# A third seven-product unit pair for the first panel pairs of two down-projection parts

## Chip, core and metric

One core of one Trainium2 chip runs the kernel, with its engines PE (matmul), DVE and ACT (elementwise work) and the queues that issue transfers. The metric is device time in microseconds (us) of the whole launch.

## What is computed

A decoder trunk of two layers on 256 tokens of width 2048, everything in float32. Each layer mixes tokens (gated linear attention, then forgetting attention, both with cross-attention to 256 memory tokens) and ends in a gated MLP with a short convolution. The change lies in the MLP's second product, `@ w_down`:

```python
FFN_HIDDEN = 11 * D_MODEL // 4          # 5632

def conv_ffn(h, w_up, conv_w, conv_b, w_down):
    u = causal_dwconv(h @ w_up, conv_w, conv_b)
    a, val = split_cols(u, [FFN_HIDDEN, FFN_HIDDEN])
    return (jax.nn.silu(a) * val) @ w_down

# per layer i, after the mixer
h = rmsnorm(x, norm_ffn[i])
x = x + conv_ffn(h, ffn_w_up[i], ffn_conv_w[i], ffn_conv_b[i], ffn_w_down[i])
```

## The kernel before

**Precision by halves.** A float32 factor is split into a high half (`hi`, rounded to the type fp32r) and the rest (`lo`). A product of two such factors is three matmuls: token high by weight high, token low by weight high, token high by weight low. Each matmul has a 128x128 block of activations (one chunk of 128 channels, one half of the tokens) as stationary operand, and moves 512 columns of weights.

**Units and panels.** Weights lie in memory as panels of 512 output columns, each cut into units of two chunks: 128 x 1024 values, 512 KB. For each unit, SP's queue loads `raw` (four buffers, line 207), ACT rounds it into `whi` (three buffers, line 208), and DVE subtracts to get `wlo` (three buffers, line 217). Then PE runs the products. `passed()` counts units and runs delayed steps that are due.

**The MLP.** The 5632 hidden channels go in three parts of 16, 16 and 12 chunks (`PARTS`). For each part, up panels are multiplied first; each result is scaled by ACT, turned through device memory, and eight to nine units later `taken` does the convolution and gating and splits the channel's activations into the chunk buffers (`A` in layer 0, `B` in layer 1, tiles 0 to 15). Then come four down panels over the part's 16 chunks, so eight units each.

**Seven products instead of eight.** In the first two parts, the down panels go in pairs (f = 0, 1 and f = 2, 3) through `add_seven` and `proj_seven`. A unit of both panels of the pair (a unit pair) is a 2x2 block product: two token halves, two chunks, two panels. Done plainly it is eight block products, 24 matmuls. In the units listed in `SEVEN`, a scheme of seven products replaces it, 21 matmuls. It needs sums of weights: from the two raw tiles `r0`, `r1` of the unit pair, DVE makes `t13` and `t24` (lines 338 to 341), and `halves` splits `r0`, the second half of `r1`, `t13` and `t24` (called v0, v1, v2, v3 below; the halves of v1 are `vhi` and `vlo`). It needs sums of activations too (`forms`, made by `summed`, lines 1021 to 1031, from `sf`), which are made for every unit that is in `SEVEN[1]`. Four of the seven products have one place each in the result and share the accumulators m1, m5, m6, m7 over all seven-product units of the pair (`ps_t`, `ps_s`, `ps_o`, `ps_s` in PSUM); the other three add into the ordinary accumulators `acc`. At the pair's end, DVE adds the four `acc` and, in `more`, the combinations of the m's to the residual `x`. There are eight banks: four for `acc`, four for the m's.

**What sets the order.** Every engine runs its own list in order, and waits at semaphores. The order of the lists is made ahead by a scheduler, from program order and priorities: loads and splits are raised by `AHEAD`, raw sums by `AHEAD + 40`, so that weights are prepared before the matmuls that use them. It interleaves the units of neighbouring panels.

## Time and profile before

| | us |
|---|---|
| median of 3 runs | 2243.26 (2242.03 to 2243.55) |
| the profiled execution | 2244.32 |
| its span | 2242.5 |
| DVE busy | 1631.0 |
| ACT busy | 1288.8 |

A busy share is an average over the whole span. Whether a helper engine holds PE up is read at one place, from the order of the lists and the start times there.

### The profile page before, as it was taken

How to read it: one execution, taken by the hardware profiler on the slowest of the kernel's cores; microseconds unless marked ns; L12 is line 12 of the kernel's file. 1: busy time of each engine (PE TensorE's matmuls, PEld its weight loads, DVE VectorE, ACT ScalarE, POOL GpSimd, SP SyncE). 2: the span in 40 equal slices, each digit the busy share in tenths (PEclk: the TensorE clock that was granted, in tenths of full speed). 3: DMA queues.
4: the chain of work that ended last, by engine and by line, in shares of the span. 5: the costliest groups of instructions: out<-in, count | busy, mean ns of one | idle time of the engine just before them, and what ended most of it. 6: DMA issues, size and time to landing. Idle time of an engine off the chain costs nothing.

```text
span 2242.5 us, 29514 instructions
## 1 busy us (share of the span) xinstructions
PE 2229.0 (99%) x10276; PEld 1861.9 (83%) x10276; DVE 1631.0 (73%) x2553; ACT 1288.8 (57%) x1910; POOL 2.9 (0%) x15
## 2 busy tenths in 40 slices
PE   9999999999999999999999999999999999999998
PEld 7888888888888888888888998888888888888886
DVE  7568887667689677886776556666777967797766
ACT  7555666556565566555655555555665455654654
POOL 0000000000000000000000000000000000000000
PEclk9999999999999999999999999999999999999999
DMA  9876667677876777668787986677776678766774
GB/s 320 276 237 189 202 201 229 202 239 242 256 222 200 244 236 244 210 205 249 237 250 249 260 265 205 179 247 236 249 247 208 206 241 243 240 197 229 238 242 150
DMA packets 303773, 516.97 MB, mean 231 GB/s; under 512 B 178556, under 2 KB 187272, under 8 KB 303496
## 3 DMA queue, kind: packets, MB, share of 16 engines
q1 hardware_dynamic: 124296, 427.24, 59.1%
q10 hardware_dynamic: 179328, 87.85, 14.0%
q8 instruction: 80, 1.31, 0.3%
q14 instruction: 69, 0.57, 0.1%
HBM read 470.44 MB, written 44.58 MB: 230 GB/s over the span
## 4 chain that ended last, share of the span: by engine, by line
PE 96%; DMA 1%; DVE 1%; issue 0%; ACT 0%; SPq 0%; ACTq 0%; DVEq 0%
PE acc L229 26%; PE acc L230 26%; PE acc L233 26%; PE acc L291 12%; PE ps_s L291 1%; PE ps_o L291 1%; PE ps_t L291 1%; DMA xturned<-square 1%; PE ps_s L785 0%; DVE wlo L217 0%; PE ps_t L575 0%; PE ps_s L586 0%; PE ps_o L597 0%; DMA mt<-memt 0%; DMA raw<-wp 0%
## 5 line engine op out<-in xcount | busy, mean ns | idle before, releaser
L217 DVE TENSOR_TENSOR wlo<-raw,whi 128x1024 fp32r<-128x1024 f32 (+4 forms) x769 | 921.4, 1201 | 503.4 <-ACT whi L208 459.7
L208 ACT ACTIVATE whi<-raw 128x1024 fp32r<-128x1024 f32 (+4 forms) x769 | 799.0, 1041 | 741.1 <-PE acc L230 528.3
L229 PE MATMUL acc<-whi,B 128*128 128x512 f32 (+3 forms) x1536 | 586.2, 383 | 0.6 <-ACT whi L208 0.6
L230 PE MATMUL acc<-whi,B 128*128 128x512 f32 (+3 forms) x1536 | 584.9, 382 | 0.0
L229 PE MATMUL acc<-whi,A 128*128 128x512 f32 x1184 | 462.5, 392 | 0.9 <-ACT whi L208 0.6
L230 PE MATMUL acc<-whi,A 128*128 128x512 f32 x1184 | 461.2, 391 | 0.0
L233 PE MATMUL acc<-wlo,B 128*128 128x512 f32 (+3 forms) x1536 | 400.7, 381 | 0.0
L229 PEld LDWEIGHTS acc<-whi,B 128*128 128x128 f32 x1536 | 288.2, 188 | 51.5 <-ACT whi L208 1.1
L230 PEld LDWEIGHTS acc<-whi,B 128*128 128x128 f32 x1536 | 287.9, 188 | 49.7
L233 PEld LDWEIGHTS acc<-wlo,B 128*128 128x128 f32 x1536 | 285.6, 188 | 49.8
L233 PE MATMUL acc<-wlo,A 128*128 128x512 f32 x1184 | 318.5, 390 | 0.3 <-DVE wlo L217 0.3
L229 PEld LDWEIGHTS acc<-whi,A 128*128 128x128 f32 x1184 | 222.1, 188 | 49.2 <-ACT whi L208 2.4
L233 PEld LDWEIGHTS acc<-wlo,A 128*128 128x128 f32 x1184 | 222.1, 188 | 46.9 <-DVE wlo L217 0.7
L230 PEld LDWEIGHTS acc<-whi,A 128*128 128x128 f32 x1184 | 222.2, 188 | 46.1 <-DVE A L479 0.4
L1010 ACT ACTIVATE cv<-u,cw 128x256 f32<-128x256 f32 x176 | 96.8, 588 | 21.0 <-DMA u<-turned 21.0
L291 PE MATMUL acc<-whi,B 128*128 128x512 f32 x392 | 102.9, 390 | 0.3 <-ACT whi L208 0.3
L291 PE MATMUL acc<-whi,A 128*128 128x512 f32 x392 | 103.0, 390 | 0.0
L1011 DVE SCALAR_TENSOR_TENSOR cv<-u,cw,cv 128x256 f32<-128x256 f32 x176 | 78.4, 480 | 12.9 <-ACT cv L1010 12.9
L291 PEld LDWEIGHTS acc<-whi,B 128*128 128x128 f32 x392 | 73.5, 188 | 16.4 <-ACT whi L208 0.8
L291 PEld LDWEIGHTS acc<-whi,A 128*128 128x128 f32 x392 | 73.5, 188 | 16.1 <-ACT whi L208 0.4
L312 ACT ACTIVATE whi<-t 128x1024 fp32r<-128x1024 f32 x40 | 42.4, 1061 | 69.0 <-DVE t L341 35.3
L394 DVE STREAM_TRANSPOSE square<-scaled 128x512 f32<-128x512 f32 x122 | 79.9, 691 | 0.0
(231 smaller groups left out, 1604.0 us busy)
## 6 DMA issues: line engine op xcount, KB each, us to landing
raw<-wp SPq DMA_DIRECT2D x743, 512.0 KB, 4.3
turned<-square ACTq DMA_DIRECT2D x61, 512.0 KB, 4.3
u<-turned ACTq DMA_DIRECT2D x176, 128.0 KB, 5.1
raw<-wp SPq DMA_DIRECT2D x32, 384.0 KB, 3.5
raw<-wp SPq DMA_DIRECT2D x24, 388.0 KB, 4.6
back<-xturned ACTq DMA_DIRECT2D x64, 128.0 KB, 5.3
xturned<-square ACTq DMA_DIRECT2D x12, 512.0 KB, 4.0
back<-turned ACTq DMA_DIRECT2D x32, 128.0 KB, 4.6
```

The lines of the kernel that those rows point to most:

```text
L208: casts.append(S.activation(hi[:, s], raw[:, s], AF.Copy))
L217: V.tensor_tensor(lo[:, s], raw[:, s], hi[:, s].bitcast(F32), ALU.subtract)
L229: TE.matmul(acc[:, :n], xh, hi[:, s], start=first and j == 0, stop=False)
L230: TE.matmul(acc[:, :n], xl, hi[:, s], start=False, stop=False)
L233: TE.matmul(a, xh, ls, start=False, stop=stop)
L291: TE.matmul(a, x, w, start=k not in begun, stop=calls[k] == 0)
L312: casts.append(S.activation(hi, raw, AF.Copy))
L394: V.transpose(self.square[:, :, :, b], src.rearrange("p (c t) -> p c t", t=32))
L1010: S.activation(r, v[:, 2:], AF.Identity, bias=w[3], scale=w[2])
L1011: V.scalar_tensor_tensor(r, v[:, 1 : T + 1], w[1], r, ALU.mult, ALU.add)
```

## The change

`SEVEN` names the units in seven-product form for the first panel pair and for the second. It changes from `((3, 5), (3, 5, 7))` to `((3, 5, 7), (3, 5, 7))`: unit 7, the last of the eight, takes the seven-product form in the first pair also. This concerns two parts in each of two layers, so four places. The rest of the diff makes `proj_seven` work for other widths (`n` in place of 512), makes the shared accumulators when the first seven-product unit needs them, and moves the token sums into `token_sums`. `seven_evacuated`, `sums_of` and the argument `extra` are not used by any call.

```diff
-SEVEN = ((3, 5), (3, 5, 7))
+SEVEN = ((3, 5, 7), (3, 5, 7))
...
-    def proj_seven(keys, src, forms, evacs, pool, more, early=False):
+    def proj_seven(keys, src, forms, evacs, tiles, more, early=False):
...
-        count = len(units[0])
+        count, n = len(units[0]), units[0][0][2]
...
-        m1, m5, m6, m7 = (work(t, n) for t, n in (("t", 1), ("s", 2), ("o", 1), ("s", 2)))
         begun, calls = set(), {}
+        shared = []
...
-                        for b in range(2):
-                            evacs[i](b, acc[i][b])
+                        for b in range(2):
+                            evacs[i](b, acc[i][b][:, :n])
                 if u == count - 2 and count - 1 in forms:
                     evacs[1](1, acc[1][1])
                 continue
+            if not shared:
+                shared += [work(t, m) for t, m in (("t", 1), ("s", 2), ("o", 1), ("s", 2))]
+                for a in shared:
+                    count_calls(a, 3 * len(forms))
+            m1, m5, m6, m7 = shared
             s = forms[u]
             with tc.high_priority(offset=AHEAD + 40):
                 r0, r1 = (load(units[i][u]) for i in range(2))
-                t13, t24 = (pool.tile([P, 2, 512], F32, name=n, tag=n) for n in ("t13", "t24"))
-                V.tensor_tensor(t13[:, 0, :], r1[:, :512], r0[:, :512], ALU.subtract)
-                V.tensor_tensor(t13[:, 1, :], r1[:, 512:], r1[:, :512], ALU.subtract)
-                V.tensor_tensor(t24[:, 0, :], r1[:, 512:], t13[:, 0, :], ALU.subtract)
-                V.tensor_tensor(t24[:, 1, :], r0[:, 512:], t24[:, 0, :], ALU.subtract)
+                t13, t24 = (tiles(t, F32)[:, : 2 * n] for t in ("t13", "t24"))
+                V.tensor_tensor(t13[:, :n], r1[:, :n], r0[:, :n], ALU.subtract)
+                V.tensor_tensor(t13[:, n:], r1[:, n:], r1[:, :n], ALU.subtract)
+                V.tensor_tensor(t24[:, :n], r1[:, n:], t13[:, :n], ALU.subtract)
+                V.tensor_tensor(t24[:, n:], r0[:, n:], t24[:, :n], ALU.subtract)
             with tc.high_priority(offset=AHEAD):
-                v0 = halves(r0, NUNIT)
-                v1 = halves(r1[:, 512:], 512)
+                v0 = halves(r0)
+                v1 = halves(r1[:, n:], True)
             passed()
             emit([form(m1, token(k0, 0), *v0, 0), form(acc[0][0], token(k1, 0), *v0, 1)])
             emit([form(acc[1][0], s(3), *v1, 0)])
...
+    def token_sums(a0, a1, b0, b1, f, form):
+        V.tensor_tensor(f[:, 0, :], a1, b1, ALU.add)
+        V.tensor_tensor(f[:, 2, :], a0, a1, ALU.subtract)
+        V.tensor_tensor(f[:, 1, :], f[:, 0, :], a0, ALU.subtract)
+        V.tensor_tensor(f[:, 3, :], b0, f[:, 1, :], ALU.subtract)
+        hi, lo = form
+        S.activation(hi, f, AF.Copy)
+        V.tensor_tensor(lo, f, hi.bitcast(F32), ALU.subtract)
...
-                        add_seven(key, f, m, {u: form(forms[u]) for u in at}, sp)
+                        add_seven(key, f, m, {u: form(forms[u]) for u in at}, spare_tile)
```

With the old table, the rewritten functions give every engine the same rows in the same order as before. With the new one, the four places change alike. Three lists at the first of them (layer 0, part 0, end of the first panel pair):

**DVE**, from where its list first differs (just behind the split of `A14`). `wlo_6364` and `wlo_6382` belong to unit 6 of both panels, `wlo_6400` and `wlo_6420` to unit 7. Before:

```order
L217 TENSOR_TENSOR wlo_6364<-raw_6360,whi_6361 128x1024
L1026 TENSOR_TENSOR sf_6276<-cv1_6244,cv1_6268 128x128
L217 TENSOR_TENSOR wlo_6382<-raw_6378,whi_6379 128x1024
L476 TENSOR_TENSOR A15_99<-cv1_6268,A15_99 128x256
L1028 TENSOR_TENSOR sf_6276<-sf_6276,cv1_6244 128x128
L217 TENSOR_TENSOR wlo_6400<-raw_6396,whi_6397 128x1024
L1029 TENSOR_TENSOR sf_6276<-cv1_6268,sf_6276 128x128
L217 TENSOR_TENSOR wlo_6420<-raw_6416,whi_6417 128x1024
L1031 TENSOR_TENSOR forms2_4585<-sf_6276,forms2_4585 128x512
```

Now:

```order
L346 TENSOR_TENSOR t13_6401<-raw_6399,raw_6397 128x512
L347 TENSOR_TENSOR t13_6401<-raw_6399 128x512
L217 TENSOR_TENSOR wlo_6364<-raw_6360,whi_6361 128x1024
L315 TENSOR_TENSOR vlo_6412<-raw_6399,vhi_6411 128x512
L400 TENSOR_TENSOR sf_6276<-cv1_6244,cv1_6268 128x128
L217 TENSOR_TENSOR wlo_6382<-raw_6378,whi_6379 128x1024
L348 TENSOR_TENSOR t24_6402<-raw_6399,t13_6401 128x512
L524 TENSOR_TENSOR A15_99<-cv1_6268,A15_99 128x256
L315 TENSOR_TENSOR wlo_6408<-raw_6397,whi_6407 128x1024
L402 TENSOR_TENSOR sf_6276<-sf_6276,cv1_6244 128x128
L315 TENSOR_TENSOR wlo_6425<-t13_6401,whi_6424 128x1024
L349 TENSOR_TENSOR t24_6402<-raw_6397,t24_6402 128x512
```

The raw sums of unit 7 and its extra splits stand among unit 6's splits; the low half of v3 and the forms' low half come behind the rows shown.

**ACT**, from the split of `A14` on. Before:

```order
L475 ACTIVATE A14_98<-cv1_6244 128x256
L208 ACTIVATE whi_6379<-raw_6378 128x1024
L208 ACTIVATE whi_6397<-raw_6396 128x1024
L475 ACTIVATE A15_99<-cv1_6268 128x256
L208 ACTIVATE whi_6417<-raw_6416 128x1024
L208 ACTIVATE whi_6455<-raw_6454 128x1024
L1030 ACTIVATE forms2_4585<-sf_6276 128x512
```

Now (`whi_6407`, `whi_6424`, `whi_6434` are the high halves of v0, v2, v3; `whi_6462` is the next panel pair's unit 0):

```order
L523 ACTIVATE A14_98<-cv1_6244 128x256
L208 ACTIVATE whi_6379<-raw_6378 128x1024
L314 ACTIVATE vhi_6411<-raw_6399 128x512
L314 ACTIVATE whi_6407<-raw_6397 128x1024
L523 ACTIVATE A15_99<-cv1_6268 128x256
L314 ACTIVATE whi_6424<-t13_6401 128x1024
L314 ACTIVATE whi_6434<-t24_6402 128x1024
L208 ACTIVATE whi_6462<-raw_6461 128x1024
L405 ACTIVATE forms2_4585<-sf_6276 128x512
L1021 ACTIVATE s16_6447<-ps_t_6195 128x512
L208 ACTIVATE whi_6480<-raw_6479 128x1024
```

`whi_6434` stands behind DVE's second `t24`, and the next pair's `whi_6462` behind it.

**PE**, unit 6's low products and the start of unit 7. Before:

```order
L291 MATMUL acc_6066<-wlo_6364,A12_96 128x512
L291 MATMUL acc_6066<-wlo_6364,A13_97 128x512
L291 MATMUL acc_6067<-wlo_6364,A12_96 128x512
L291 MATMUL acc_6067<-wlo_6364,A13_97 128x512
L291 MATMUL acc_6066<-whi_6397,A14_98 128x512
L291 MATMUL acc_6066<-whi_6397,A15_99 128x512
L291 MATMUL acc_6067<-whi_6397,A14_98 128x512
L291 MATMUL acc_6067<-whi_6397,A15_99 128x512
L291 MATMUL acc_6066<-whi_6397,A14_98 128x512
L291 MATMUL acc_6067<-whi_6397,A14_98 128x512
L291 MATMUL acc_6068<-wlo_6382,A12_96 128x512
L291 MATMUL acc_6068<-wlo_6382,A13_97 128x512
```

Now; ahead of the rows shown stand, in the place where the list first differs, two matmuls of v0 on `ps_t` and the first one of `wlo_6364`:

```order
L291 MATMUL acc_6066<-wlo_6364,A13_97 128x512
L291 MATMUL acc_6067<-wlo_6364,A12_96 128x512
L291 MATMUL acc_6067<-wlo_6364,A13_97 128x512
L291 MATMUL acc_6066<-whi_6407,A15_99 128x512
L291 MATMUL acc_6068<-wlo_6382,A12_96 128x512
L291 MATMUL acc_6068<-wlo_6382,A13_97 128x512
L291 MATMUL acc_6069<-wlo_6382,A12_96 128x512
L291 MATMUL acc_6069<-wlo_6382,A13_97 128x512
L291 MATMUL acc_6066<-whi_6407,A15_99 128x512
L291 MATMUL ps_t_6195<-wlo_6408,A14_98 128x512
L291 MATMUL acc_6066<-wlo_6408,A15_99 128x512
L291 MATMUL acc_6067<-whi_6434,A15_99 128x512 x2
```

Behind them follow the next panel pair's first eight matmuls, all of `whi_6462`; the seven form's remaining products come after those. So the two matmuls of v3 stand 14 matmuls behind the place where the list first differs.

More of the change, by code (lines that the diff above doesn't have):

```diff
@@ L268, in proj_two @@
                         evacs[i](b, acc[i][b][:, : units[i][0][2]])
-    def proj_seven(keys, src, forms, evacs, pool, more, early=False):
+    def proj_seven(keys, src, forms, evacs, tiles, more, early=False):
         units = [where[k] for k in keys]
-        count = len(units[0])
+        count, n = len(units[0]), units[0][0][2]
         base = min(min(u[1]) for u in units[0])
         acc = [[pacc.tile([P, 512], F32, name="acc", tag="acc") for _ in range(2)] for _ in keys]
-        m1, m5, m6, m7 = (work(t, n) for t, n in (("t", 1), ("s", 2), ("o", 1), ("s", 2)))
         begun, calls = set(), {}
+        shared = []
         def form(a, x, hi, lo, c):
-            s = slice(c * 512, (c + 1) * 512)
+            s = slice(c * n, (c + 1) * n)
             out = []
@@ L290, in emit @@
                 calls[k] -= 1
-                TE.matmul(a, x, w, start=k not in begun, stop=calls[k] == 0)
+                TE.matmul(a[:, :n], x, w, start=k not in begun, stop=calls[k] == 0)
                 begun.add(k)
@@ L300, in proj_seven @@
                 count_calls(acc[i][b], 6 * len(plain))
-        for a in (m1, m5, m6, m7, acc[0][0], acc[1][0], acc[0][1]):
+        for a in (acc[0][0], acc[1][0], acc[0][1]):
             count_calls(a, 3 * len(forms))
@@ L305, in token, with halves @@
             return [src[kc - base][:, i, b * P : (b + 1) * P] for i in range(2)]
-        def halves(raw, w):
-            if w == NUNIT:
-                hi, lo = (wpool.tile([P, w], F32R, name=n, tag=n, bufs=3) for n in ("whi", "wlo"))
-            else:
-                hi, lo = (pool.tile([P, w], F32R, name=n, tag=n) for n in ("vhi", "vlo"))
+        def halves(raw, single=False):
+            w = n if single else 2 * n
+            if single:
+                hi, lo = (tiles(t, F32R) for t in ("vhi", "vlo"))
+            else:
+                hi, lo = (wpool.tile([P, NUNIT], F32R, name=t, tag=t, bufs=3) for t in ("whi", "wlo"))
+            hi, lo = hi[:, :w], lo[:, :w]
             casts.append(S.activation(hi, raw, AF.Copy))
@@ L317, in load @@
             off, kcs, n = unit
-            raw = wpool.tile([P, NUNIT], F32, name="raw", tag="raw", bufs=4)
-            loads.append(nc.sync.dma_start(raw, wp[off : off + P * NUNIT].rearrange("(p n) -> p n", p=P)))
+            w = len(kcs) * n
+            raw = wpool.tile([P, NUNIT], F32, name="raw", tag="raw", bufs=4)[:, :w]
+            loads.append(nc.sync.dma_start(raw, wp[off : off + P * w].rearrange("(p n) -> p n", p=P)))
             return raw
@@ L348, in proj_seven @@
             with tc.high_priority(offset=AHEAD):
-                v2 = halves(t13.rearrange("p c n -> p (c n)"), NUNIT)
+                v2 = halves(t13)
             emit([form(m5, s(0), *v2, 0), form(m7, s(2), *v2, 1)])
             with tc.high_priority(offset=AHEAD):
-                v3 = halves(t24.rearrange("p c n -> p (c n)"), NUNIT)
+                v3 = halves(t24)
             passed()
@@ L362, in proj_seven, with seven_evacuated, more, evac @@
             more(m1, m5, m6, m7)
+    def seven_evacuated(keys, src, forms, evacs, tiles):
+        n = where[keys[0]][0][2]
+        extra = {}
+        def more(m1, m5, m6, m7):
+            u, v, w = (tiles(t, F32)[:, :n] for t in ("s16", "s165", "s1675"))
+            m1, m5, m6, m7 = (m[:, :n] for m in (m1, m5, m6, m7))
+            S.activation(u, m1, AF.Copy)
+            V.tensor_tensor(u, u, m6, ALU.add)
+            V.tensor_tensor(v, u, m5, ALU.add)
+            V.tensor_tensor(u, u, m7, ALU.add)
+            V.tensor_tensor(w, u, m5, ALU.add)
+            extra.update({(0, 0): m1, (1, 0): v, (0, 1): u, (1, 1): w})
+        def evac(i):
+            return lambda b, a: evacs[i](b, a, extra[i, b])
+        proj_seven(keys, src, forms, [evac(i) for i in range(2)], tiles, more, True)
+    def sums_of(src, chunks, f, h, form):
+        for c, k in enumerate(chunks):
+            V.tensor_tensor(h[:, c, :], *(src[k][:, i, :].bitcast(F32) for i in range(2)), ALU.add)
+        (a0, a1), (b0, b1) = ([h[:, c, b * P : (b + 1) * P] for b in range(2)] for c in range(2))
+        token_sums(a0, a1, b0, b1, f, form)
+    def token_sums(a0, a1, b0, b1, f, form):
[6 more added lines that the diff above has]
+        V.tensor_tensor(lo, f, hi.bitcast(F32), ALU.subtract)
     def turned(pool, bank, width, col):
@@ L422, in to_features, with evac @@
         held = []
-        def evac(b, a):
+        def evac(b, a, extra=None):
             if not held:
@@ L435, in evac @@
                     S.activation(o, i, AF.Copy, scale=s()[:, b : b + 1])
+                    if extra is not None:
+                        V.scalar_tensor_tensor(o, extra, s()[:, b : b + 1], o, ALU.mult, ALU.add)
             held[0].put(b, e)
@@ L445, in to_values, with evac @@
         held = []
-        def evac(b, a):
+        def evac(b, a, extra=None):
             e = tp.tile([P, 512], F32, name="scaled", tag="scaled", bufs=2)
             S.activation(e[:, :width], a[:, :width], AF.Copy, scale=norm.col()[:, b : b + 1])
+            if extra is not None:
+                V.scalar_tensor_tensor(e, extra, norm.col()[:, b : b + 1], e, ALU.mult, ALU.add)
             held.append(e)
@@ L965, in add_out, with add_seven @@
             proj_tm((*key, f), src, add_panel(f, then), spare if f == 3 else None)
-    def add_seven(key, f, src, forms, pool, then=None):
+    def add_seven(key, f, src, forms, tiles, then=None):
         x0, x1 = x[f], x[f + 1]
@@ L979, in more @@
             V.tensor_tensor(x1, x1, m5.unsqueeze(1).to_broadcast([P, 2, 512]), ALU.add)
-        proj_seven([(*key, g) for g in (f, f + 1)], src, forms, [add_panel(g, then) for g in (f, f + 1)], pool, more,
+        proj_seven([(*key, g) for g in (f, f + 1)], src, forms, [add_panel(g, then) for g in (f, f + 1)], tiles, more,
                    then is not None)
@@ L997, in ffn, with spare_tile @@
             held = []
+            def spare_tile(name, dtype):
+                return sp.tile([P, 512 if name in ("vhi", "vlo") else NUNIT], dtype, name=name, tag=name)
             def form(t):
@@ L1022, in summed @@
             def summed(form):
-                h0, h1 = (natural(h) for h in held)
+                ab = [natural(h)[:, :, b] for h in held for b in range(2)]
                 held.clear()
-                f = sp.tile([P, 4, P], F32, name="sf", tag="sf")
-                V.tensor_tensor(f[:, 0, :], h0[:, :, 1], h1[:, :, 1], ALU.add)
-                V.tensor_tensor(f[:, 2, :], h0[:, :, 0], h0[:, :, 1], ALU.subtract)
-                V.tensor_tensor(f[:, 1, :], f[:, 0, :], h0[:, :, 0], ALU.subtract)
-                V.tensor_tensor(f[:, 3, :], h1[:, :, 0], f[:, 1, :], ALU.subtract)
-                S.activation(form[:, 0, :, :], f, AF.Copy)
-                V.tensor_tensor(form[:, 1, :, :], f, form[:, 0, :, :].bitcast(F32), ALU.subtract)
+                token_sums(*ab, sp.tile([P, 4, P], F32, name="sf", tag="sf"), [form[:, h, :, :] for h in range(2)])
             def panel(j, base, slack=0):
@@ L1062, in ffn @@
                     for f, at in zip((0, 2), SEVEN):
-                        add_seven(key, f, m, {u: form(forms[u]) for u in at}, sp)
+                        add_seven(key, f, m, {u: form(forms[u]) for u in at}, spare_tile)
                     continue
                 if LAST:
-                    add_seven(key, 0, m, {u: form(forms[u]) for u in LAST}, sp, then)
+                    add_seven(key, 0, m, {u: form(forms[u]) for u in LAST}, spare_tile, then)
                 sums.close()
```

## The prediction

> **What bounds the kernel now.** I read the page first, then PE's waits, then the four places one after another. The page's chain and PE's list of waits (columns: waits in total, count, longest) say:

> ```profile
> PE 2229.0 (99%) x10276; PEld 1861.9 (83%) x10276; DVE 1631.0 (73%) x2553; ACT 1288.8 (57%) x1910; POOL 2.9 (0%) x15
> PE 96%; DMA 1%; DVE 1%; issue 0%; ACT 0%; SPq 0%; ACTq 0%; DVEq 0%
> PE ps_o L174 <- DVE B L171: 1.4, 1, 1.4
> ...
> PE acc L233 <- DVE wlo L217: 0.3, 1, 0.3
> ```

> PE is the whole story: the seven rows of its waits add to 4.1 us of a span of 2242.5. So a matmul taken away is worth its full pitch, and any wait put into PE's list costs its full length, since nothing later gives it back. DVE's 73% is an average; what counts is DVE at the four places. Busy time by stretch (PE, PEld, DVE, ACT) around the end of the first panel pair:

> ```profile
> 664.00:674.00 10.00, 10.00 (x45) 8.07 (x43) 10.00 (x15) 5.93 (x8) 0.00 (x0) 1.00 0.62 208
> 674.00:684.00 10.00, 10.00 (x45) 8.03 (x44) 8.68 (x15) 5.30 (x7) 0.00 (x0) 1.00 0.64 207
> 684.00:694.00 10.00, 10.00 (x46) 8.29 (x45) 10.00 (x14) 4.34 (x5) 0.00 (x0) 1.00 0.67 216
> 922.00:932.00 10.00, 10.00 (x45) 8.23 (x44) 10.00 (x16) 6.38 (x9) 0.00 (x0) 1.00 0.63 205
> 1716.00:1726.00 10.00, 9.44 (x40) 6.88 (x38) 10.00 (x16) 6.12 (x8) 0.00 (x0) 1.00 0.61 209
> 1974.00:1984.00 10.00, 10.00 (x45) 8.23 (x44) 10.00 (x17) 6.40 (x9) 0.00 (x0) 1.00 0.60 209
> ```

> In the ten microseconds ahead of each place DVE is busy without a gap: units 3 and 5 in seven form, and the last up panels' convolution and forms, fall together there. The change puts more DVE work at just that point.

> **What is taken away.** Each place loses 24 - 21 = 3 matmuls. The existing seven-product unit (unit 3 here) and a plain stretch behind it give both prices:

> ```profile
> 658.50 0.39 PE L291 MATMUL ps_t<-whi,A 128*128 128x512 f32 x1
> ...
> 663.36 3.79 PE L291 MATMUL acc<-whi,A 128*128 128x512 f32 x16
> 666.98 1.07 PE L291 MATMUL acc<-wlo,A 128*128 128x512 f32 x4
> ```

> Plain: 16 matmuls in 666.98 - 663.36 = 3.62 us, 0.226 each, so 24 take 5.43. Seven form: its 21 run from 658.50 to 663.36, 4.86. The gain is 0.57 a place, 2.3 us in four places (2.7 if the three are counted at 0.226). This is the most that the change can bring beyond the waits that exist.

> **What is added on DVE, and when PE needs it.** Four raw sums of 512, the 512-wide `vlo`, and three splits of 1024 in place of two. The order of the lists up to the split of `A14` is unchanged, so DVE reaches the first changed instruction when it now starts `wlo_6364`. DVE's list there, and ACT's answer to a second `t24`:

> ```profile
> 668.97 0.69 DVE L341 TENSOR_TENSOR t<-raw,t 128x512 f32<-128x512 f32 x1
> 669.58 1.22 DVE L313 TENSOR_TENSOR wlo<-raw,whi 128x1024 fp32r<-128x1024 f32 x1
> ...
> 674.98 1.23 DVE L217 TENSOR_TENSOR wlo<-raw,whi 128x1024 fp32r<-128x1024 f32 x1
> 676.12 0.29 DVE L1026 TENSOR_TENSOR sf<-cv,cv 128x128 f32<-128x128 f32 x1
> 676.32 1.23 DVE L217 TENSOR_TENSOR wlo<-raw,whi 128x1024 fp32r<-128x1024 f32 x1
> 677.45 0.42 DVE L476 TENSOR_TENSOR A<-cv,A 128x256 fp32r<-128x256 f32 x1
> 677.79 0.29 DVE L1028 TENSOR_TENSOR sf<-sf,cv 128x128 f32<-128x128 f32 x1
> ...
> 669.78 1.06 ACT L312 ACTIVATE whi<-t 128x1024 fp32r<-128x1024 f32 x1 [3.03 <-DVE t L341]
> 673.14 2.20 ACT L208 ACTIVATE whi<-raw 128x1024 fp32r<-128x1024 f32 x2 [0.57 <-PE acc L291]
> ```

> Start to start, a 512-wide one takes 0.61 (668.97 to 669.58), a 1024-wide split 1.13, a 256-wide one 0.34, a 128-wide one 0.20. From 674.98 to the end of the second `t24` the new list has 12 instructions: four splits (4.52), two `t13`, `vlo` and the first `t24` (2.42), two `sf` (0.40), `A15` (0.34), and the last `t24` at its full 0.69. That is 8.37. ACT starts 0.12 behind it (668.97 + 0.69 to 669.78) and rounds v3's high half in 1.06. So `whi_6434` is there 9.55 us behind DVE's start.

> PE reaches the place where its list differs when it now starts unit 6's low products. The four places' two starts:

> ```profile
> 677.61 1.07 PE L291 MATMUL acc<-wlo,A 128*128 128x512 f32 x4
> 932.57 1.22 DVE L217 TENSOR_TENSOR wlo<-raw,whi 128x1024 fp32r<-128x1024 f32 x1
> 935.98 1.07 PE L291 MATMUL acc<-wlo,A 128*128 128x512 f32 x4
> 1726.79 1.23 DVE L217 TENSOR_TENSOR wlo<-raw,whi 128x1024 fp32r<-128x1024 f32 x1
> 1729.40 1.07 PE L291 MATMUL acc<-wlo,B 128*128 128x512 f32 x4
> 1984.32 1.23 DVE L217 TENSOR_TENSOR wlo<-raw,whi 128x1024 fp32r<-128x1024 f32 x1
> 1987.76 1.07 PE L291 MATMUL acc<-wlo,B 128*128 128x512 f32 x4
> ```

> PE is 2.63, 3.41, 2.61 and 3.44 us behind DVE's start, and has 14 matmuls (3.16 us) in front of v3's. It arrives 5.8 to 6.6 us behind DVE's start, and the weights come at 9.55. **First wait:** 3.76, 2.98, 3.78 and 2.95 us, together 13.5. Part of it falls ahead of v3, at `wlo_6408`, which the same DVE list brings late; the sum is the same.

> **Second wait:** ACT rounds `whi_6462` behind `whi_6434`; 1.10 a piece (2.20 for two), against two matmuls of v3 (0.45) in front of it. 0.6 a place, 2.4 us. All matmuls behind these two waits in PE's list are queued, the next pair's eight first, though their accumulators are free.

> **Third:** `whi_6480` (next pair, unit 0, second panel) takes the buffer of v2's high half, which PE holds until the forms' low products are through, so cast, split and DVE's addition of the old accumulator follow each other just when PE asks. From the rows: the cast 1.06 against about three matmuls left, the split's 1.13 against four matmuls, the addition 0.61 against two. Each is short by 0.2 to 0.3: 0.8 a place at most, nothing if the buffer comes free sooner. No row shows it; I take 0.6, 2.4 us, since the first two waits have the same order of work.

> **At nothing:** the forms of unit 7 exist already, for the second pair. Transfers keep their sequence. `r1` of unit 7 must have landed by DVE's first sum:

> ```profile
> 670.82 0.33 SPq L207 DMA_DIRECT2D raw<-wp  x1
> DMA to landing us min/median/max: 3.2/4.1/4.9
> ```

> At the median it lands at 674.9, just in time for 674.98; at the longest 0.7 late, 2.9 us in four places; that end goes into the range. The raw tiles of unit 7 are held until the last `t24`, so the fourth next load starts at about 683.2 and lands four later; PE asks for it after 692. The new placement of the m accumulators and the unused helpers issue nothing.

> [...] The rows' starts are closer together than their durations, so the trace decides against charging them whole.

> **Sum:** 13.5 + 2.4 + 2.4 - 2.3 = +16.0. The profiled execution's own 2244.32 (1.8 outside the span) becomes 2260.3; it lies 1.06 above the median, so I say 2259 for the runs.

> **Rivals.**
> *Not slower: PE has enough in front.* The same DVE list ran for unit 5 in the stretch 664 to 674, DVE full, and PE lost nothing in three of the four places (at 1716 it lost 0.56). If DVE's lead at the place were 6.4 us, in place of 2.6 to 3.4, the first wait would vanish, and the others with it, as ACT would follow: 2243.3 - 2.3 = 2241. Against it: DVE has no gap ahead of the place, so there is no lead to be found. 9%.
> *Half of it:* the waits that follow the first vanish, and some DVE instruction ahead of it is in truth covered: first wait 2 us a place, 8 - 2.3 = +5.7, 2249. For it: small differences of a few tenths in 12 instructions. 8%.
> *PE's clock falls after each wait.* The first matmuls of the launch, behind PE's longest wait, are slow:

> ```profile
> 1.45 3.61 PE L174 MATMUL ps_o<-B 128*128 128x512 f32 x8 [1.45 <-DVE B L171]
> ```

> Eight in 3.61, against 1.81 at 0.226: 1.8 us lost. After each of four waits that is 7.2 more: 2266. Against it, the wait is in two pieces (some 0.9, then 2.0 to 2.7) with matmuls between. 8%. [...]
> *The change does nothing:* the lists show that it does; no chance.

> **How the numbers follow.** Forecast 75%: +12 to +19, from the third wait at nothing and the gain at 2.7 to late loads, so 2255 to 2262 alone. The range reaches to the half case below and to the clock case above: 2249 to 2266. A change of 0.2% (4.5 us) is about what a measurement can tell from none. Slower by more: forecast, clock, and most of the half case, 88%. Within: nearly all of the not-slower case, as its 2.3 us are 0.1%, and a little of the half case, 9%. Faster by more needs the whole gain and PE's existing 4.1 us of waits, 3%.

> **What would show it.** PE's waits grow from 4.1 to about 22 us, led by `acc` of the seven products on ACT's rounding of `t` (v3), with next `ps_t` on the low half of v0, once at each place; PE has 12 matmuls fewer; DVE is full from each place until some 8 us later. No wait of PE on `t`'s rounding would refute the first step; eight slow matmuls after a wait would show the clock; waits on `raw` would show late loads. If these four places show less than 1.5 us of wait each, the forecast is wrong.

## The result and the profile after

The kernel became slower: 2263.49 us (2257.72 to 2266.38 in four runs) against 2242.66 (four runs, one more than in the table ahead), a ratio of 1.0084 with a 95% interval of 1.0073 to 1.0096, so about 21 us. The forecast was 2259. The profiled execution of after is the shortest of the four, 2257.72 us with a span of 2255.9; it is 13.4 us above the profiled one of before. The runs of before lie within 1.5 us, those of after within 8.7. The mean granted clock is 0.997 in the shortest run of after and 0.995 and 0.996 in the two longest; it was 0.999 in before.

The page's line of busy times, its chain by engine, and PE's waits of after (total, count, longest):

```profile
PE 2232.5 (99%) x10264; PEld 1861.8 (83%) x10264; DVE 1646.1 (73%) x2577; ACT 1293.5 (57%) x1918; POOL 2.9 (0%) x15
PE 91%; DVE 4%; DMA 2%; issue 1%; ACT 1%; SPq 0%; ACTq 0%; DVEq 0%
...
PE acc L291 <- ACT whi L314: 9.1, 4, 2.4
PE ps_o L174 <- DVE B L171: 1.4, 1, 1.4
PE acc L229 <- ACT whi L208: 1.3, 3, 0.8
PE acc L291 <- DVE wlo L217: 0.7, 1, 0.7
PE acc L291 <- ACT whi L208: 0.6, 3, 0.2
PE ps_t L291 <- DVE wlo L315: 0.5, 1, 0.5
PE acc L233 <- DVE wlo L217: 0.2, 1, 0.2
```

PE has 12 matmuls fewer. The first row is the forecast's first wait, four times, of `acc` on the rounding of `t`. The chain now passes through DVE, DMA and ACT for 4, 2 and 1%, where before PE had 96%. The first place, row by row (DVE's first raw sum; PE at the point where its list differs; DVE's last raw sum; ACT's rounding of it, and of the next pair's unit; v3's two matmuls; the next pair's first eight):

```profile
673.50 0.69 DVE L346 TENSOR_TENSOR t<-raw 128x512 f32<-128x512 f32 x1 [0.53 <-DVE A L524]
677.11 0.62 PE L291 MATMUL ps_t<-whi,A 128*128 128x512 f32 x2
681.20 0.68 DVE L349 TENSOR_TENSOR t<-raw,t 128x512 f32<-128x512 f32 x1
682.00 1.06 ACT L314 ACTIVATE whi<-t 128x1024 fp32r<-128x1024 f32 x1 [4.04 <-DVE t L349]
682.96 1.04 ACT L208 ACTIVATE whi<-raw 128x1024 fp32r<-128x1024 f32 x1
683.11 0.73 PE L291 MATMUL acc<-whi,A 128*128 128x512 f32 x2 [2.37 <-ACT whi L314]
684.06 2.11 PE L291 MATMUL acc<-whi,A 128*128 128x512 f32 x8 [0.21 <-ACT whi L208]
```

From DVE's first sum to v3's first matmul are 683.11 - 673.50 = 9.61 us; the other three places give 9.61, 9.60 and 9.61. PE comes 3.61 us behind DVE's start (3.07, 4.21, 3.95 at the others). Now the same matmuls at the second and the fourth place, and the stretches around the first, second and fourth (after the busy times: granted clock, DMA share, GB/s):

```profile
944.86 4.22 PE L291 MATMUL acc<-whi,A 128*128 128x512 f32 x10 [2.38 <-ACT whi L314]
...
2002.69 3.48 PE L291 MATMUL acc<-whi,B 128*128 128x512 f32 x8 [0.21 <-ACT whi L208]
```

```profile
674.00:684.00 10.00, 7.47 (x31) 5.16 (x29) 10.00 (x16) 4.48 (x7) 0.00 (x0) 1.00 0.57 186
944.00:954.00 10.00, 9.14 (x32) 7.09 (x33) 7.92 (x12) 5.80 (x7) 0.00 (x0) 0.83 0.39 120
2004.00:2014.00 10.00, 10.00 (x40) 8.05 (x39) 7.54 (x10) 4.41 (x5) 0.00 (x0) 0.88 0.44 114
```

Eight matmuls behind the wait take 2.11 us at the first place and 3.48 at the fourth, and the granted clock of that stretch is 0.88 in place of 1.00. So PE's clock fell at the second (0.83) and the fourth place (0.88), and not at the first and the third (1.00 in 674 to 684 and in 1736 to 1746).

**Where the time went.** I measured in the trace, from the start of the first matmul of a part's two panel pairs to the start of the last, and counted in it PE's waits, and what consecutive starts of 512-column matmuls lie apart beyond 0.2265 us each (waits taken out, differences under 0.01 us left out):

| place | before: stretch, waits, pitch | after: stretch, waits, pitch |
|---|---|---|
| 1 | 84.29, 0, 0.29 | 86.87, 2.58, 0.87 |
| 2 | 84.05, 0, 0 | 88.92, 2.91, 2.60 |
| 3 | 85.36, 0.63, 0.79 | 86.33, 2.27, 0.57 |
| 4 | 84.03, 0, 0 | 89.15, 3.20, 2.48 |

Together the stretches grew by 13.54 us, all of the difference between these two executions. Waits brought 10.96 - 0.63 = 10.3, slower pitch 6.52 - 1.08 = 5.4, the fewer matmuls -2.3: 13.4. Of the pitch, some 0.5 a place is PE starting again after a wait (places 1 and 3); the rest, 1.5 to 2 us each, is the clock at places 2 and 4.

### The profile page after: what moved, and what is told of

Its sections match the earlier page's. It is cut to its first block, busy times and chain, and to the rows that moved or that the text cites. A ratio compares the mean times of both kernels' runs of the same rounds, so it can differ in the third digit from the quotient of the medians.

```text
span 2255.9 us, 29526 instructions
## 1 busy us (share of the span) xinstructions
PE 2232.5 (99%) x10264; PEld 1861.8 (83%) x10264; DVE 1646.1 (73%) x2577; ACT 1293.5 (57%) x1918; POOL 2.9 (0%) x15
## 3 DMA queue, kind: packets, MB, share of 16 engines
q10 hardware_dynamic: 179328, 87.85, 13.8%
## 4 chain that ended last, share of the span: by engine, by line
PE 91%; DVE 4%; DMA 2%; issue 1%; ACT 1%; SPq 0%; ACTq 0%; DVEq 0%
PE acc L229 26%; PE acc L230 26%; PE acc L233 26%; PE acc L291 8%; DVE wlo L217 1%; DMA raw<-wp 1%; PE ps_s L291 1%; DVE wlo L315 1%; DMA xturned<-square 1%; PE ps_s L833 0%; PE ps_o L291 0%; ACT whi L208 0%; DVE vlo L315 0%; PE ps_t L291 0%; PE ps_t L623 0%
## 5 line engine op out<-in xcount | busy, mean ns | idle before, releaser
L217 DVE TENSOR_TENSOR wlo<-raw,whi 128x1024 fp32r<-128x1024 f32 (+4 forms) x761 | 910.4, 1199 | 496.7 <-ACT whi L208 448.9
L208 ACT ACTIVATE whi<-raw 128x1024 fp32r<-128x1024 f32 (+4 forms) x761 | 789.6, 1040 | 713.0 <-PE acc L230 514.8
L233 PE MATMUL acc<-wlo,B 128*128 128x512 f32 (+3 forms) x1536 | 400.6, 381 | 0.0
L233 PEld LDWEIGHTS acc<-wlo,B 128*128 128x128 f32 x1536 | 285.7, 188 | 49.7
L233 PE MATMUL acc<-wlo,A 128*128 128x512 f32 x1184 | 318.5, 390 | 0.2 <-DVE wlo L217 0.2
L233 PEld LDWEIGHTS acc<-wlo,A 128*128 128x128 f32 x1184 | 222.1, 188 | 46.7 <-DVE wlo L217 0.7
L291 PE MATMUL acc<-whi,A 128*128 128x512 f32 x368 | 99.3, 396 | 5.0 <-ACT whi L314 4.8
L291 PE MATMUL acc<-whi,B 128*128 128x512 f32 x368 | 99.4, 396 | 4.8 <-ACT whi L314 4.4
L314 ACT ACTIVATE whi<-t 128x1024 fp32r<-128x1024 f32 x48 | 50.5, 1060 | 90.5 <-DVE t L349 44.7
L291 PEld LDWEIGHTS acc<-whi,A 128*128 128x128 f32 x368 | 69.8, 191 | 21.6 <-ACT whi L314 5.6
L291 PEld LDWEIGHTS acc<-whi,B 128*128 128x128 f32 x368 | 69.6, 190 | 21.4 <-ACT whi L314 5.2
```

The costliest lines, as they stand in the source:

```text
L208: casts.append(S.activation(hi[:, s], raw[:, s], AF.Copy))
L217: V.tensor_tensor(lo[:, s], raw[:, s], hi[:, s].bitcast(F32), ALU.subtract)
L233: TE.matmul(a, xh, ls, start=False, stop=stop)
L291: TE.matmul(a[:, :n], x, w, start=k not in begun, stop=calls[k] == 0)
L314: casts.append(S.activation(hi, raw, AF.Copy))
```

## The experiments

"Before" was run again beside each group of them, at a median of 2243.5 to 2243.7 us, and the ratios are against that. "After" is the changed kernel; each edit is made to it.

### The same kernel again

> The changed kernel once more, for its spread. Theory A (PE waits for the high half of v3, and in some of the four places its clock falls to half for some microseconds afterwards): the runs spread again over some 8 us, 2257 to 2267, and the granted clock of a run, 0.995 to 0.997, is lower the longer it is; the profile shows a first wait of 2 to 3.4 us in each place and eight to ten slow matmuls behind some of them. Rival B (the spread comes from loads that land early or late): the clock doesn't go with the time, and the profile shows waits on raw tiles.

Measured: 2264.8 us (2263.0 to 2265.62), ratio 1.0096 (1.0081 to 1.0112). The profiled execution is longer than that of after by 5.3 us. Its four places, v3's and the next pair's matmuls:

```profile
683.21 4.11 PE L291 MATMUL acc<-whi,A 128*128 128x512 f32 x10 [2.38 <-ACT whi L314]
...
946.32 4.00 PE L291 MATMUL acc<-whi,A 128*128 128x512 f32 x10 [2.37 <-ACT whi L314]
...
1744.88 3.32 PE L291 MATMUL acc<-whi,B 128*128 128x512 f32 x7 [0.21 <-ACT whi L208]
...
2007.79 4.02 PE L291 MATMUL acc<-whi,B 128*128 128x512 f32 x10 [2.38 <-ACT whi L314]
```

All four are slow: the granted clock is 0.88 in 684 to 694, and 0.83 in 944 to 954, 1744 to 1754 and 2004 to 2014. By the same count as above, waits are 11.8 us more than in before and pitch 8.3 more; the stretches grew by 18.0 us of the 18.7 between the two executions. So the same program loses the clock at two places in one execution and at four in another. Of the 5.3 us between this execution and that of after, 3.0 are pitch, 1.5 longer waits in the stretches, and the rest lies outside them.

Two points of theory A did not come: these four runs lie within 2.6 us, not 8, and their mean clock is 0.996 in each, so it does not rank them. Of rival B a small part is true: ahead of its first raw sums DVE sat idle until `r1` had landed, 1.6 us in the four places, against 0.9 in after.

### Matmuls that fill the wait

```diff
+            if u == count - 1 and keys[0][-1] == 0:
+                zero, many = wpool.tile([P, P], F32R, name="zero", tag="zero", bufs=1), FILL
+                nc.gpsimd.memset(zero.bitcast(F32), 0.0)
+                a, w = acc[0][1], v0[0]
+                for _ in range(many):
+                    TE.matmul(a[:, :n], zero, w[:, :n], start=False, stop=False)
             emit([form(m6, s(1), *v3, 0), form(acc[0][1], token(k1, 1), *v3, 1)])
```

With FILL = 10:

> Ten matmuls with a stationary block of zeros are put ahead of v3's two in PE's list at each of the four places; they add nothing to the sum, and take 2.27 us a place at 0.227 each. Theory A: they fill the wait (2.2 to 3.4 us) without lengthening it, the clock stays up, so the time is that of the waits alone: 2243 + 10.9 + 2.5 - 2.3 = 2254 (2252 to 2257), with a spread under 3 us and a clock of 0.999. Without a clock effect: as the changed kernel, 2258 to 2266. If there were no wait of PE's own there to fill: 9 us longer than the changed kernel, 2267 to 2275.

Measured: 2262.55 us (2261.92 to 2263.97), ratio 1.0086 (1.0072 to 1.01), a miss by 8 us. DVE's first sum, v3's and the next matmuls at the first place:

```profile
676.52 0.69 DVE L347 TENSOR_TENSOR t<-raw 128x512 f32<-128x512 f32 x1 [1.28 <-DMA raw<-wp]
...
686.13 0.73 PE L292 MATMUL acc<-whi,A 128*128 128x512 f32 x2 [1.41 <-ACT whi L315]
687.08 2.96 PE L292 MATMUL acc<-whi,A 128*128 128x512 f32 x8 [0.22 <-ACT whi L209]
```

Here DVE's first sum itself waited 1.28 us for the load of `r1`; the chain to v3 is 9.61 us again, so ten matmuls were too few, 4.7 us of waits on v3 were left, and the clock still fell at this place (0.83 granted in 684 to 694). A transfer elsewhere took 1.7 us of PE's time. So this run cannot separate the clock from the waits. With FILL = 18:

> Edit: 18 matmuls with a zero stationary operand (18 x 0.226 = 4.07 us a place, 16.3 us in four) stand ahead of v3's at the four places, in place of 10 in the run before; nothing else differs from after. They use no late data, so PE is busy in place of waiting. Theory A (part of the loss is PE's clock falling after the waits, 1.6 to 1.8 us a fall): no wait over 1 us is left at the places, no slice shows a lowered clock there, and the time is 2243.5 - 2.3 + 16.3 + 0 to 3 for the waits behind them = 2257.5 to 2260.5, with runs that lie within 2 us of each other: shorter than after by some 4 to 7 us though PE does 16.3 us more work. Theory B (the clock plays no part, and the run spread of after is something else): the waits of 10.9 us are replaced by 16.3 us of work, so 5 us longer than after's 2264.8, about 2268 to 2270.

Measured: 2259.26 us (2258.35 to 2260.66), ratio 1.0072 (1.0059 to 1.0084). The stretches behind the four places:

```profile
684.00:694.00 10.00, 9.99 (x44) 7.63 (x43) 9.63 (x13) 5.97 (x7) 0.00 (x0) 1.00 0.47 151
944.00:954.00 10.00, 10.00 (x46) 8.21 (x45) 9.08 (x14) 4.82 (x6) 0.20 (x1) 1.00 0.54 188
1746.00:1756.00 10.00, 10.00 (x46) 8.25 (x45) 9.67 (x12) 5.54 (x6) 0.00 (x0) 1.00 0.63 204
2004.00:2014.00 10.00, 10.00 (x46) 8.20 (x45) 8.74 (x12) 6.09 (x7) 0.00 (x0) 1.00 0.41 131
```

PE is hardly idle there, the clock stays at 1.00, and PE's list has no wait left at the four places. 2243.74 - 2.3 + 16.3 (72 matmuls) is 2257.7, the measured time less 1.6. PE does 16.3 us of extra work in place of 10 to 12 us of waits, and the kernel is 4 to 5.5 us shorter than after (2263.5 and 2264.8), with runs 2.3 us apart. Theory A's range holds this, B's does not: the clock's part of the loss is shown.

### DVE's list lightened

First, the raw sums of unit 7 on GpSimd in place of DVE:

```diff
-                V.tensor_tensor(t13[:, :n], r1[:, :n], r0[:, :n], ALU.subtract)
+                E = nc.gpsimd if u == count - 1 and keys[0][-1] == 0 else V
+                E.tensor_tensor(t13[:, :n], r1[:, :n], r0[:, :n], ALU.subtract)
...
```

> At the four new places alone, the four raw sums (t13 and t24) go to GpSimd, which is idle, in place of DVE. Theory A (DVE's list of 12 instructions makes v3 late): 2.4 us leave that list and v3's high half no longer stands behind it, the first and second wait go nearly away (under 0.5 us a place), no slow matmuls: 2241 to 2244. Rival C (v3 is late for its buffer, for ACT or for the load, DVE does not matter): 2254 or more, the waits of 2 to 3 us are still there. If a sum takes over 2 us on GpSimd: waits of up to 2 us a place, 2246 to 2252.

Measured: 2271.54 us (2267.32 to 2276.94), ratio 1.0127 (1.0109 to 1.0144), worse than after. GpSimd and DVE at the first place:

```profile
675.37 1.77 POOL L347 TENSOR_TENSOR t<-raw 128x512 f32<-128x512 f32 x1 [255.62 <-DMA raw<-wp]
676.00 1.70 DVE L315 TENSOR_TENSOR vlo<-raw,vhi 128x512 fp32r<-128x512 f32 x1
...
677.11 1.74 POOL L348 TENSOR_TENSOR t<-raw 128x512 f32<-128x512 f32 x1
677.62 1.37 DVE L401 TENSOR_TENSOR sf<-cv,cv 128x128 f32<-128x128 f32 x1
678.80 1.32 POOL L349 TENSOR_TENSOR t<-raw,t 128x512 f32<-128x512 f32 x1
...
678.91 2.29 DVE L217 TENSOR_TENSOR wlo<-raw,whi 128x1024 fp32r<-128x1024 f32 x1
```

DVE's `sf` takes 1.37 us where it took 0.29, and each of DVE's three ends only 0.1 to 1.1 us after the GpSimd sum beside it (677.14, 678.85, 680.12). The sums left DVE's list and DVE became no freer, so theory A's range failed without A being tested. Only the open range of rival C holds the time, and not for C's reason.

Second, v3 split from `t13`, without the two sums of `t24`:

```diff
-                V.tensor_tensor(t24[:, :n], r1[:, n:], t13[:, :n], ALU.subtract)
-                V.tensor_tensor(t24[:, n:], r0[:, n:], t24[:, :n], ALU.subtract)
+                short = u == count - 1 and keys[0][-1] == 0
+                if not short:
+                    V.tensor_tensor(t24[:, :n], r1[:, n:], t13[:, :n], ALU.subtract)
+                    V.tensor_tensor(t24[:, n:], r0[:, n:], t24[:, :n], ALU.subtract)
...
-                v3 = halves(t24)
+                v3 = halves(t13 if short else t24)
```

> Edit: unit 7 of the first panel pairs leaves out the two last raw sums (t24); v3 is split from t13, so four products have other weights; every matmul of after stays. DVE's list to the last operand of v3 is two instructions (1.3 us) shorter, and ACT's rounding of v3 no longer stands behind the last of them. Theory A (DVE's chain t13, splits, t24, then ACT's rounding sets the wait): the rounding of v3 is there some 3 us earlier, the first wait of 2.2 to 3.4 us vanishes or falls under 0.8, the clock stays at 0.999: 2244 (2241 to 2249). Theory B (the wait comes from late loads of unit 7's raw tiles): the waits stay within 1 us of what they were, 2257 to 2265.

Measured: 2259.66 us (2258.6 to 2261.88), ratio 1.0075 (1.0061 to 1.0089). The forecast wait on the rounding is gone, as expected, and the gain did not come. PE at the second place:

```profile
945.52 0.50 PE L291 MATMUL acc<-wlo,A 128*128 128x512 f32 x1 [1.58 <-DVE wlo L315]
946.21 3.62 PE L291 MATMUL acc<-whi,A 128*128 128x512 f32 x8 [0.19 <-DVE x L1006]
```

Now v3's low half, on DVE, is late by 1.2 to 1.6 us at each place (5.9 in four), because the scheduler put its product ahead of the next pair's matmuls, and the clock fell once (0.83 granted in 944 to 954). The wait moved down the list. Neither theory had this: B's range holds the time, but PE does not wait for a load here.

Third, in the first two parts, the convolution of the last four chunks without its oldest tap, then of the last eight without two of its four taps (the first of the two edits is shown):

```diff
-                    V.scalar_tensor_tensor(r, v[:, :T], w[0], r, ALU.mult, ALU.add)
+                    if j - base < 12:
+                        V.scalar_tensor_tensor(r, v[:, :T], w[0], r, ALU.mult, ALU.add)
```

> Edit: in after, the convolution of the last four chunks of the first two parts leaves out its oldest tap: eight DVE instructions of 128x256 a place (0.40 us start to start, 3.2 us), all ahead of unit 7's raw sums; matmuls, loads and splits are all there, the order at the place is arranged anew a little. Theory A (DVE's whole list in the ten to twenty microseconds ahead of unit 7 is full, and the new sums come on top of it: throughput, not the place of one instruction): 3.2 us less DVE work there is about the first wait (2.2 to 3.4 us in after), so unit 7's sums start that much earlier against PE, the waits at the four places fall under 0.8 us each, no clock fall: 2243 (2241 to 2247). Theory B (v3's chain of load, sums and rounding is late by its own length, however busy DVE was ahead of it): the waits stay within 1 us of after's, 2255 to 2265.

Measured: 2249.93 us (2246.94 to 2251.89), ratio 1.0026 (1.0017 to 1.0034), between the two theories' ranges. Part of what is left stands in the second panel pairs: `ps_o` waits there for the rounding of `t`, 2.8 us in seven waits.

> Edit: in after, the convolution of the last eight chunks of the first two parts leaves out two of its four taps: 32 DVE instructions of 128x256 a part (0.40 us start to start, 12.8 us), most of them ahead of unit 7's raw sums by up to 30 us; matmuls, loads and splits are all there. Theory A (DVE's backlog at unit 7 is the whole loss, and what was left in the run with eight instructions fewer, waits of 0.4 to 0.8 us in the second panel pairs, is the rest of the same backlog): the waits left are under 0.3 us a place, no clock fall, and the 2.3 us of the fewer matmuls come out: 2242 (2240.5 to 2245). Theory B (DVE idles earlier, waiting for loads, so work taken away 10 to 30 us ahead does not help; the 4.2 us of unit 7 themselves fill the stretch from unit 7 to the second pair's unit 3): the waits of the second pairs stay, 2247 to 2250.

Measured: 2243.45 us (2240.35 to 2245.57), ratio 0.9997 (0.9988 to 1.0006). The first place in the run with four chunks thinned (first sum, ACT's rounding of v3, PE's first matmul of v3):

```profile
675.07 0.69 DVE L346 TENSOR_TENSOR t<-raw 128x512 f32<-128x512 f32 x1 [0.63 <-DMA raw<-wp]
...
681.87 1.06 ACT L314 ACTIVATE whi<-t 128x1024 fp32r<-128x1024 f32 x1 [1.95 <-DVE t L349]
...
683.47 0.40 PE L291 MATMUL ps_o<-whi,forms 128*128 128x512 f32 x1
```

and in the run with eight:

```profile
673.31 0.69 DVE L346 TENSOR_TENSOR t<-raw 128x512 f32<-128x512 f32 x1 [2.38 <-DMA raw<-wp]
...
680.53 1.06 ACT L314 ACTIVATE whi<-t 128x1024 fp32r<-128x1024 f32 x1 [3.01 <-DVE t L349]
...
681.76 0.39 PE L291 MATMUL ps_o<-whi,forms 128*128 128x512 f32 x1
```

At the four places PE waits for v3 in neither run, and in neither did the clock fall there (1.00 granted from 674 to 714, 0.999 over each execution). But it is not for the reason that I wrote: the sums don't start earlier, as they wait 0.63 and 2.38 us for the load of `r1`, and at this place v3 is rounded at 682.9 and 681.6, against 683.1 in after. Two other things changed. The chain from the first sum to v3's high half is shorter, 7.86 and 8.28 us in place of 9.56, since `A15`, the split of v2 and one or two `sf` no longer stand in it (in the second run the low half of the forms does). And PE has 21 matmuls from where its list differs up to v3, where it had 14: the activations' forms of chunks 14 and 15 are ready sooner, and the scheduler puts the products of v1 and v2 ahead of v3's. How much each of the two brought was not separated.

Of the 2.3 us that the matmuls save, the second run shows its share at three places: the stretches are 84.06, 83.37 and 83.50 us against 84.29, 84.05 and 84.03. At the third place two waits of 1.3 and 1.2 us, one in each panel pair, made it 86.68 against 85.36, and the total is level with before. The range of theory A holds it, that of B does not. Before was not thinned in the same way; as its PE waits 4.1 us in all, that is the most that fewer taps could bring it by shorter waits.

### Other places for the third unit

Unit 1 in place of unit 7 in the first pairs (the tile of activation sums is shared with unit 7 of the second pair), then units 1, 3, 5 in both pairs:

```diff
-SEVEN = ((3, 5, 7), (3, 5, 7))
+SEVEN = ((1, 3, 5), (3, 5, 7))
```

> Edit: the third seven-product unit pair of the four first panel pairs is unit 1 in place of unit 7; the second panel pairs keep 3, 5, 7; the same count of matmuls as after. Theory A (the loss comes from the place: DVE's full list behind the end of the up panels' convolution makes v3 late at unit 7): at unit 1 DVE was only 6.0 of 10 us busy in the trace of before (644 to 654), so the raw sums are ready in time, the 0.57 us a place are kept, and the time is 2241 (2240 to 2244), PE's waits stay under 6 us, granted clock 0.999. Theory B (a third unit's raw sums cost PE about 3 us wherever they stand, since v3 always comes behind the same chain of load, sums, rounding): 2254 to 2264, with waits of acc on the rounding of t at four places. Theory C (loads: the DMA share was 0.79 to 0.88 around units 0 to 2, so the two extra early loads come late): waits on raw, 2245 to 2250.

Measured: 2253.41 us (2252.85 to 2256.94), ratio 1.0049 (1.0037 to 1.0062): between the theories. The waits are not at unit 1 but 20 us later, at unit 5:

```profile
672.81 0.68 DVE L349 TENSOR_TENSOR t<-raw,t 128x512 f32<-128x512 f32 x1
672.95 0.73 PE L291 MATMUL ps_s<-wlo,forms 128*128 128x512 f32 x2 [1.05 <-DVE wlo L315]
...
674.72 0.50 PE L291 MATMUL ps_o<-whi,forms 128*128 128x512 f32 x1 [1.04 <-ACT whi L314]
```

In before the last sum of unit 5 started at 668.97 (quoted in the prediction), here at 672.81. The free time of DVE at units 1 to 3 (6.0 of 10 us busy) was spent at unit 1, and work that had stood there comes later: from unit 3's first sum to unit 5's last, DVE has 27 instructions in place of 21, with 0.56 us of idle time in place of 1.72. That this makes unit 5 late is read from the lists; no run isolates it. The waits come in pieces of about 1 us, and the clock fell at one place of four (at 1731.60 five matmuls take 2.33 us; 0.998 granted over the execution).

> Edit: units 1, 3, 5 in both panel pairs, in place of 3, 5, 7; the same count of matmuls as after. Theory A: the first pairs are as in the run with unit 1 in the first pairs alone; in the second pairs unit 1 falls into the stretch in which DVE also adds the first pair's results (8.4 to 10 of 10 us busy in before at 684 to 704), so a wait of 0 to 2 us a place can come there: 2241 to 2249. Theory B (a third unit costs about 3 us in a first pair wherever it stands): 2254 or more.

Measured: 2267.79 us (2265.09 to 2269.08), ratio 1.0107 (1.0094 to 1.0121). The second pairs wait too: `ps_o` on the rounding of `t`, 9.1 us in 11 waits, and the clock fell at two places (0.998 granted over the execution, 0.999 in before). Theory A's range fails; B's holds it, though the waits are not in the first pairs alone.

The third part, with unit 3, and with units 1 and 3, of its first panel pair in seven-product form, and the first two parts as in before:

```diff
-LAST = ()
+LAST = (1, 3)
```

> Edit: the first panel pairs keep units 3 and 5 as before; in place of their third unit, the first panel pair of the third part (12 chunks, six units) gets units 1 and 3 in seven-product form, in both layers: 4 unit pairs, the same 12 matmuls fewer as in after, at places where DVE is busy 6.3 to 7.1 of 10 us in before (1115 to 1145) in place of 8.7 to 10. Theory A (the change loses because of DVE's full list at its place): no new waits of PE over 0.5 us, gain 4 x 0.57 = 2.3 us: 2241.5 (2240.5 to 2243.5). Theory B (any further seven-product unit costs PE more than it gains): 2247 or more.

> Edit: as the run with units 1 and 3 in the third part, with unit 3 alone there: 2 unit pairs, 6 matmuls fewer than before. Theory A: gain 2 x 0.57 = 1.1 us: 2242.5 (2241.5 to 2244). Theory B: 2245 or more.

Measured: 2258.07 us (2256.24 to 2258.88), ratio 1.0061 (1.0048 to 1.0073), and 2249.35 us (2247.47 to 2253.51), ratio 1.0025 (1.0016 to 1.0034). Both are slower, against theory A. PE in the run with two units:

```profile
1144.13 1.19 PE L291 MATMUL acc<-whi,A 128*128 128x512 f32 x4 [1.50 <-ACT A L523]
1148.89 4.64 PE L291 MATMUL acc<-whi,A 128*128 128x512 f32 x10 [3.56 <-ACT A L523]
```

PE waits for activations here: DVE's convolution of the part's last chunks stands among the raw sums, splits and result sums of the seven form. The clock fell behind the second of these waits, in both layers (0.66 granted in 1145 to 1155, 0.995 over the execution). I had counted only the average of DVE's busy share there, 6.3 to 7.1 of 10. In these runs the four stretches of the first two parts are 84.0 to 85.0 us, so the rewritten functions alone cost nothing.

### The third unit of the second pairs taken away

```diff
-SEVEN = ((3, 5, 7), (3, 5, 7))
+SEVEN = ((3, 5), (3, 5))
```

> The seven form is taken away from unit 7 of the second panel pair also, so that both pairs have units 3 and 5 only. This measures what a third unit pair in last place gains where DVE isn't full: theory (0.57 us a place): 2.3 us slower than before, 2245 (2244 to 2246). If the third unit costs a wait there too: same as before or faster, 2240 to 2243.

Measured: 2245.71 us (2244.47 to 2249.73), ratio 1.0016 (1.0007 to 1.0024), 2.2 us slower than before for 12 matmuls more. The runs fall into two groups, six from 2244.5 to 2245.7 and five from 2248.8 to 2249.7; the profiled execution is of the upper one, and its trace shows a wait of 2.0 us and a fall of the clock at 1495 (0.998 granted over the execution), far from the four places. The stretches give the price without that: 84.59 and 84.60 us at the second and the fourth place, against 84.05 and 84.03 in before, where PE has neither waits nor slower pitch there. So the worth of a unit pair in seven form, where nothing waits, is 0.54 to 0.57 us a place, as forecast. None of the versions is clearly faster than before.

## Why the prediction was right, and where not

- **Sign and range.** Slower, inside 2249 to 2266. The narrower 2255 to 2262 for the forecast alone did not hold the median of 2263.5; it is inside 2249 to 2266 because a rival given 8% had set the upper end. That the sum came within 5 us is luck: two errors stood against each other, waits of 18.3 us where 10.3 came, and PE's clock left out of the sum.
- **Gain, 2.3 us.** Right (0.54 to 0.57 us a place in the run without the second pairs' third unit).
- **"`whi_6434` is there 9.55 us behind DVE's start."** Right: 9.61 at v3's first matmul in all four places. Counting instructions start to start was what made it right. The durations of the rows of before charged whole (nine of the 12 at 1.23 or 0.69 us, the others at 0.42 and 0.29) add to 9.4 us in place of 8.37, which would have been 1 us long at each place.
- **First wait, 13.5 us.** The mechanism is right, the size was not: 9.6 (9.1 on v3, 0.5 at the low half of v0). The term that failed is PE's distance behind DVE, "2.63, 3.41, 2.61 and 3.44 us"; it was 3.61, 3.07, 4.21, 3.95. I took it from the rows of before as if the change left it alone. It accounts for 2.8 of the 3.9 us that did not come. Most of the rest is counting: the profile's wait begins at the modelled end of the last matmul, 0.4 us behind its start, where I charged 0.226. At the first place DVE's list ran earlier in after already 20 us ahead, where a load came sooner; DVE's first sum of unit 3 there, in before and in after:

```profile
652.38 0.69 DVE L338 TENSOR_TENSOR t<-raw 128x512 f32<-128x512 f32 x1 [1.48 <-DMA raw<-wp]
```

```profile
651.08 0.69 DVE L346 TENSOR_TENSOR t<-raw 128x512 f32<-128x512 f32 x1 [0.43 <-DMA raw<-wp]
```

- **Second wait, 2.4 us.** 0.6. ACT starts its two roundings 0.96 apart (682.00, 682.96), not 1.10, and v3's two matmuls take longer after the wait than the 0.45 charged.
- **Third wait, 2.4 us.** None is in the list. The bound at nothing was the true one, and "the same order of work" was no reason for 0.6. By the figures given there, the three steps are short by 0.38, 0.22 and 0.16, not by 0.2 to 0.3 each; the sum of 0.8 is right.
- **Loads "just in time".** Right, closer than told. In after `r1` landed at 673.42, 935.17, 1731.03 and 1992.01, only 0.08 to 0.18 us ahead of DVE's first sum, for which DVE had been idle 0.53, 0.29, 0 and 0.10 us (the row of 673.50 above names `A`, but that was done at 672.97). An earlier landing at these places could have started the sums at most 0.9 us sooner in all. In the filled and thinned runs DVE waited 0.6 to 2.4 us for it at the first place. The load is issued when DVE has split unit 5 out of its raw tile (at the first place that ends at 668.70, the load starts at 668.72 and takes 4.7 us), so DVE's list and the load are one chain.
- **"PE's clock falls after each wait", 8%.** The price (1.8 us a place) was about right, the chance, an estimate of mine, far too low: the clock fell at two places of four in the profiled execution, at four of four in the next. It is the part of the loss that the sum lacked, 5.4 us of pitch in one and 8.3 in the other, and part of why the runs lie from 2258 to 2266. "Against it, the wait is in two pieces" was no protection: at the second place it came in pieces of 0.53 and 2.38 and the clock fell (0.83 granted in 944 to 954). Waits that come to 2.1 to 3.0 us a place were followed by a fall at six of eight places in the two executions. That the same program loses two or four agrees with the grid shown in the last section.
- **Not slower; half of it.** Neither came. What was said against the first, that there is no lead to be found, holds for after; the thinned runs show that PE's own work in front of v3 was the other way to cover the wait.
- **What would show it.** PE's waits grew from 4.1 to 13.8 us, not to about 22, led by the row that was named; the low half of v0 made PE wait at one place of four. DVE was busy 9.0 to 10.0 of 10 us there, as told.

## What to carry to other kernels

A helper engine whose list is full for twenty microseconds had no free place in any run here: new work was paid for where its next result falls due, even units later, and an average busy share of 60 to 70% does not show that. Weigh what an edit saves on the bound engine (0.57 us) against the time from the new chain's first input to its last operand (9.6 us), less the work that the bound engine has ready in front of it (here 14 matmuls, 3.2 us, and a lead of 3 to 4). And add to a wait of PE of 2 us or more the price of a fall of the clock, 1.5 to 1.8 us, times its chance: six of eight places fell. By the figures of the next section (in after and its repeat, falls behind windows with about 2.2 us or more of idle time, none in after behind 1.48 or less), a single wait of 2.4 us brings one in four to eight cases of ten, an estimate with the window's edge anywhere.

## What the hardware did that was not expected

```profile
678.70:682.11 3.41, 2.03 (x8) 1.00 0.87 297
682.11:685.52 3.41, 2.20 (x8) 1.00 0.53 169
941.53:944.94 3.41, 0.81 (x3) 1.00 0.75 270
944.94:948.35 3.41, 3.41 (x8) 0.50 0.41 144
1999.66:2003.07 3.41, 1.12 (x4) 1.00 0.70 247
2003.07:2006.48 3.41, 3.41 (x10) 0.50 0.38 79
```

At the first place an edge of the grid cuts the wait in two, so no window has much idle time; at the other two nearly all of it lies in one. In after the two windows with 2.60 and 2.29 us of idle time were followed by a fall; the next, 1.48 us at the third place and 1.38 and 1.21 at the first, were not. Before has no window with 1 us or more of it between the first rise and PE's last matmuls. In the repeat of after each place has about 2.2 us or more of idle in one window, and all four fell. The grid lay elsewhere against the kernel there: at the first place the fall began at about 683.0 (0.95 granted in 674 to 684), with v3's matmuls at 683.21, where after has an edge at 682.11, with v3's at 683.11. So whether a wait is cut differed from one execution to the other. A fall costs 1.5 to 1.8 us, as some eight matmuls start 0.43 us apart in place of 0.2265 (eight fill the 3.41 us from 944.94).

**DVE was slower beside GpSimd's sums.** In the run with the raw sums on GpSimd, three of DVE's instructions, of 0.29 to 1.22 us elsewhere, took 1.37 to 2.29, each ending 0.1 to 1.1 us behind a GpSimd sum. What held them was not shown.
